# Adaptive max pooling: most loads and the large stores issued from GpSimd as one packet per DMA engine

## The chip, the core and the metric

The kernel runs on one core of a Trainium2 chip. A core has several engines with instruction streams of their own. Three matter here: VectorE (DVE in the profile) computes, SyncE (SP) only issues transfers, and GpSimd (POOL) can do both. Data moves between the device memory (HBM) and the on-chip memory (SBUF, 128 partitions) by DMA: an engine issues one instruction, and sixteen DMA engines do the copying. The profile counts what these move in packets, by queue; each issuing engine has a queue of its own (q1 is SyncE's, q10 is ScalarE's).

The metric is the device time of one execution in microseconds. The kernel before takes 335.21 us, the median of three runs (334.77 to 335.26).

## The reference

```python
x: (32, 256, 4096) float32, output_size = 256
for i in range(output_size):
    start = int(i * length / output_size)
    end = int((i + 1) * length / output_size)
    result[:, :, i] = np.max(x[:, :, start:end], axis=-1)
```

4096 / 256 is 16, so each output is the maximum of 16 neighbouring inputs. 134.2 MB are read and 8.4 MB written.

## The kernel before

All of `x` is seen as one list of 2,097,152 windows of W = 16 floats. Each of the 128 partitions handles 16,384 windows (`total`). The work is split in two groups of consecutive windows, `group_a` and `group_b`, and each group in loads. The first load is small (`FIRST`, 128 windows a partition). Then come nine loads in the first group, eight of 1024 windows a partition and one of 1020, and seven in the second, six of 1024 and one of 900. The small first load and sixteen large ones are thus seventeen loads. A load of 1024 windows is 64 KB a partition, 8 MB over all.

The loads land in one SBUF buffer, `ring`, that holds two of them and two gaps of 152 windows (`GAP`). A load's place is worked out from its number (lines 93 to 95): even loads go to the lower half, odd ones to the upper half, and every second use of a half is moved up by the gap. The maximum is taken by `pooled` (line 54), one VectorE reduce at line 56, called twice for a load: first a large part of 872 windows, then a small part of 152. The order is chosen such that the load after next, which goes to the same half but shifted, overlaps only the part that is reduced first (lines 98 to 101). It can therefore start as soon as the large part has been reduced, before the small one is.

Results are collected in the SBUF buffer `kept` until the end. They leave in three stores: one for each group from `kept`, issued by SyncE in the last lines (117), and a small one for the last load's 900 windows, whose results overwrite used places of `ring` (`last_kept`). That small one is issued by ScalarE (line 114).

The order of work on each engine is that of the source. The framework adds semaphore waits where one instruction needs another's data or place. SyncE's stream is: the small load (line 87), two large loads that wait for nothing but the start, fourteen large loads that each wait for VectorE's large reduce of the load two before (line 96), and the two stores (line 117). The first store needs nothing that is late when its turn comes; the second needs the reduces of the second group. GpSimd does four tiny memsets at the start and nothing more.

Of the kernel before, what the change touches and what calls it, by code (L numbers as in the profile page):

```python
# [1 line left out]

# [4 lines left out]


@with_exitstack
def kernel(  # L10
    ctx: ExitStack,
    tc: tile.TileContext,
    x: bass.AP,
    output_size: bass.AP,
    out: bass.AP,
):

    nc = tc.nc
    P = nc.NUM_PARTITIONS
    fp32 = mybir.dt.float32

    B, C, L = x.shape
    O = int(output_size)  # L30
    assert L % O == 0, (L, O)
    W = L // O
    total = B * C * O // P
    assert B * C * O % P == 0

    CHUNK = 1024
    GAP = 152
    FIRST = 128
    LOADS_A, LOADS_B = 9, 6

    LESS = 4
    group_a = [FIRST] + [CHUNK] * (LOADS_A - 1) + [CHUNK - LESS]
    last = total - sum(group_a) - LOADS_B * CHUNK
    group_b = [CHUNK] * LOADS_B + [last]
    assert 0 < last and last * (W + 1) <= CHUNK * W

    pool = ctx.enter_context(tc.tile_pool(name="pool", bufs=1))
    ring = pool.tile([P, 2 * (CHUNK + GAP) * W], fp32, tag="ring", name="ring")
    kept = pool.tile([P, total - last], fp32, tag="kept", name="kept")

    xw = x.flatten_outer_dims().rearrange("r (o w) -> (r o) w", w=W)
    ow = out.flatten_outer_dims().rearrange("r o -> (r o)")

    def pooled(dst, at, n):

        nc.vector.reduce_max(  # L56
            out=dst,
            in_=ring[:, at * W : (at + n) * W].rearrange("p (n w) -> p n w", w=W),
            axis=mybir.AxisListType.X,
        )  # L60

    taken = 0

    def group(n):

        nonlocal taken
        span = slice(taken * P, (taken + n) * P)
        taken += n
        return (
            xw[span].rearrange("(p n) w -> p (n w)", p=P),  # L70
            ow[span].rearrange("(p n) -> p n", p=P),
        )

    stores = []
    n_loads = 0
    base = 0
    for g, loads in enumerate((group_a, group_b)):
        xg, og = group(sum(loads))
        a = sum(loads) if g == 0 else 0
        for n in loads:  # L80
            if g == 0:
                a -= n
            xn = xg[:, a * W : (a + n) * W]
            dst = kept[:, base + a : base + a + n] if n != last else None
            if n == FIRST:

                nc.sync.dma_start(  # L87
                    out=ring[:, CHUNK * W : (CHUNK + n) * W], in_=xn
                )
                pooled(dst, CHUNK, n)  # L90
            else:

                low = n_loads % 2 * (CHUNK + GAP)
                moved = n_loads // 2 % 2
                at = low + moved * GAP
                nc.sync.dma_start(out=ring[:, at * W : (at + n) * W], in_=xn)
                if n != last:
                    cut = CHUNK - GAP if moved else GAP
                    parts = [(0, cut), (cut, n)]
                    for u, v in parts if moved else parts[::-1]:  # L100
                        pooled(dst[:, u:v], at + u, v - u)
                else:
                    end = (at + CHUNK) * W
                    last_kept = ring[:, end - n : end]
                    pooled(last_kept, at, n)
                n_loads += 1
            if g:
                a += n
        full = a - last if g else sum(loads)
        stores.append((og[:, 0:full], kept[:, base : base + full]))  # L110
        base += full
    assert taken == total

    nc.scalar.dma_start(out=og[:, full : full + last], in_=last_kept)
    tc.no_sync_barrier()
    for dst, src in stores:
        nc.sync.dma_start(out=dst, in_=src)


# [1 line left out]
_INS = ['x', 'output_size']  # L121
_OUTS = [((32, 256, 256), 'float32')]

_NUMBERS = {'output_size': 256}


# [26 lines left out]
```

## Time and profile before

| what | value |
|---|---|
| median of three runs | 335.21 us (334.77 to 335.26) |
| span of the profiled execution | 333.1 us |
| VectorE busy | 276.5 us (83%), 32 reduces |
| GpSimd busy | 0.2 us, 4 memsets |
| moved by DMA | 142.61 MB, mean 428 GB/s |
| SyncE's queue q1 | 2736 packets, 142.15 MB, 98.8% of sixteen engines' span |
| ScalarE's queue q10 | 144 packets, 0.46 MB, 0.3% |
| one large reduce, one small | 14.69 us, 2.68 us |

The profiled execution's own time is given as its span, from the first to the last thing that the profiler recorded; the runs' times also hold what lies around the span. A line of instructions names the engine, the line in the source, the operation, what is written and read, and how often. "SPq" is an issue on SyncE's queue. For a DMA issue, the time of the instruction is only that of issuing; "landing" is the time from issue until the semaphore tells that the data is there. An idle time in brackets is that of the engine just before the instruction, and behind the arrow stands what ended it.

### The profile page before, as it was taken

Reading aid. Unit: us, or ns where it says so; the run is one execution under the profiler, and the core shown is the slowest. Engines: PE = TensorE matmul, PEld = TensorE weight load, DVE = VectorE, ACT = ScalarE, POOL = GpSimd, SP = SyncE. Lnnn points to the kernel's source line nnn. Section 1 sums busy time; section 2 is a strip of 40 time slices with the busy share of each in tenths; the row PEclk is TensorE's granted clock in tenths of the full one; section 3 lists DMA queues with packets and bytes.
Section 4 is the critical chain, followed back from the end, with each engine's and each line's share of the span. In section 5 each row is a group of like instructions: output and inputs, shape, how many; then the busy total and the mean of one; then the engine's idle time right before and its main releaser. Section 6 shows DMA issues by size and latency. Waiting matters only on the chain.

```text
span 333.1 us, 113 instructions
## 1 busy us (share of the span) xinstructions
DVE 276.5 (83%) x32; POOL 0.2 (0%) x4
## 2 busy tenths in 40 slices
DVE  2009979797997979799797979979797998979993
POOL 0000000000000000000000000000000000000000
DMA  9898989899898989899898989899898989899997
GB/s 378 378 504 378 504 378 504 378 449 433 378 504 378 504 378 504 378 441 441 384 494 377 504 378 504 378 456 425 386 496 378 504 378 504 378 458 443 393 395 330
DMA packets 2880, 142.61 MB, mean 428 GB/s; under 512 B 320, under 2 KB 320, under 8 KB 448
## 3 DMA queue, kind: packets, MB, share of 16 engines
q1 hardware_dynamic: 2736, 142.15, 98.8%
q10 hardware_dynamic: 144, 0.46, 0.3%
HBM read 134.22 MB, written 8.39 MB: 428 GB/s over the span
## 4 chain that ended last, share of the span: by engine, by line
DMA 57%; DVE 36%; DVEq 5%; issue 0%; SPq 0%
DMA ring<-in_x_dram 57%; DVE kept L56 36%; DVEq L148 5%; SPq L87 0%
## 5 line engine op out<-in xcount | busy, mean ns | idle before, releaser
L56 DVE TENSOR_REDUCE kept<-ring 128x152 f32<-128x2432 f32 (+3 forms) x31 | 261.4, 8473 | 51.5 <-DMA ring<-in_x_dram 51.5
L56 DVE TENSOR_REDUCE ring<-ring 128x900 f32<-128x14400 f32 x1 | 15.1, 15143 | 0.0
L134 POOL MEMSET const-bfloat16-1.0<- 128x1 bf16 x1 | 0.1, 103 | 0.0
L134 POOL MEMSET const-uint8-127<- 128x1 uint8 x1 | 0.1, 102 | 0.0
L134 POOL MEMSET const-float32-0.0<- 128x1 f32 x1 | 0.1, 100 | 0.2 <-issue 0.2
L134 POOL MEMSET const-float32-1.0<- 128x1 f32 x1 | 0.1, 99 | 0.0
## 6 DMA issues: line engine op xcount, KB each, us to landing
ring<-in_x_dram SPq DMA_DIRECT2D x1, 8160.0 KB, 23.9
ring<-in_x_dram SPq DMA_DIRECT2D x1, 7200.0 KB, 21.7
out_dram<-kept SPq DMA_DIRECT2D x1, 4670.0 KB, 32.4
out_dram<-kept SPq DMA_DIRECT2D x1, 3072.0 KB, 18.2
ring<-in_x_dram SPq DMA_DIRECT2D x1, 1024.0 KB, 4.7
out_dram<-ring ACTq DMA_DIRECT2D x1, 450.0 KB, 4.2
ring<-in_x_dram SPq DMA_DIRECT2D x14, 24.0
```

The source lines that it names most:

```text
L56: nc.vector.reduce_max(out=dst, in_=ring[:, at * W : (at + n) * W].rearrange("p (n w) -> p n w", w=W), axis=mybir.AxisListType.X,)
L134: nc = _bacc.Bacc("TRN2", target_bir_lowering=False, num_devices=1)
L148: with _tile.TileContext(nc) as tc:
```

## The change

```diff
@@ -93,7 +93,11 @@
                 low = n_loads % 2 * (CHUNK + GAP)
                 moved = n_loads // 2 % 2
                 at = low + moved * GAP
-                nc.sync.dma_start(out=ring[:, at * W : (at + n) * W], in_=xn)
+                dst_ring = ring[:, at * W : (at + n) * W]
+                if n_loads < 2:
+                    nc.sync.dma_start(out=dst_ring, in_=xn)
+                else:
+                    nc.gpsimd.dma_start(out=dst_ring, in_=xn, single_packet=True)
                 if n != last:
                     cut = CHUNK - GAP if moved else GAP
                     parts = [(0, cut), (cut, n)]
@@ -114,7 +118,7 @@
     nc.scalar.dma_start(out=og[:, full : full + last], in_=last_kept)
     tc.no_sync_barrier()
     for dst, src in stores:
-        nc.sync.dma_start(out=dst, in_=src)
+        nc.gpsimd.dma_start(out=dst, in_=src, single_packet=True)
```

`n_loads` counts the large loads from zero. The small load and large loads 0 and 1 are still issued by SyncE. Large loads 2 to 15 and the two stores from `kept` are issued by GpSimd, with the flag that makes the share of each DMA engine one packet. Sizes, places, the reduces and the order among the moved transfers are as before; the waits of each moved instruction are the same as they were on SyncE. ScalarE's small store is unchanged.

## The prediction, made before the changed kernel was run

> **What bounds the kernel now.** I read the page first (busy shares, the slices, the queues, the chain), then the order of time on VectorE, SyncE's waits, and last the transfers stretch by stretch.
>
> From the page: its engine shares, slices, queues, chain and DMA issues.
>
> ```profile
> span 333.1 us, 113 instructions
> DVE 276.5 (83%) x32; POOL 0.2 (0%) x4
> ...
> DMA packets 2880, 142.61 MB, mean 428 GB/s; under 512 B 320, under 2 KB 320, under 8 KB 448
> ...
> q1 hardware_dynamic: 2736, 142.15, 98.8%
> q10 hardware_dynamic: 144, 0.46, 0.3%
> ...
> DMA 57%; DVE 36%; DVEq 5%; issue 0%; SPq 0%
> ...
> ring<-in_x_dram SPq DMA_DIRECT2D x14, 24.0
> ```
>
> VectorE is busy 83% of the span, so it waits; q1, SyncE's queue, is busy 98.8% of sixteen engines' time. q1 carried 19 transfers in 2736 packets, 144 each, nine per DMA engine: eight of data (the full loads' are 64 KB) and one under 512 B, which ends the transfer (320 = 20 transfers x 16 engines).
>
> The instructions in order of time (start, length, what, and in brackets the idle time before):
>
> ```profile
> 0.73 0.38 SPq L87 DMA_DIRECT2D ring<-in_x_dram  x1
> ...
> 5.44 2.29 DVE L56 TENSOR_REDUCE kept<-ring 128x128 f32<-128x2048 f32 x1 [5.44 <-DMA ring<-in_x_dram]
> 24.78 17.28 DVE L56 TENSOR_REDUCE kept<-ring 128x872 f32<-128x13952 f32 x2 [17.05 <-DMA ring<-in_x_dram]
> 44.13 17.28 DVE L56 TENSOR_REDUCE kept<-ring 128x872 f32<-128x13952 f32 x2 [2.07 <-DMA ring<-in_x_dram]
> 63.48 17.28 DVE L56 TENSOR_REDUCE kept<-ring 128x872 f32<-128x13952 f32 x2 [2.07 <-DMA ring<-in_x_dram]
> 82.83 17.28 DVE L56 TENSOR_REDUCE kept<-ring 128x872 f32<-128x13952 f32 x2 [2.08 <-DMA ring<-in_x_dram]
> ```
>
> I number the full loads 0, 1, 2 and on. They land at 24.78, 44.13, 63.48, 82.83: one each 19.35 us, with 2.07 us of VectorE idle ahead of it. A load is 8192 KB, 8.389 MB, so 433.5 GB/s. The beat is the transfer's, as long as the next load is queued before the one under way ends. Whether it is, SyncE's waits and its next issue tell:
>
> ```profile
> SPq L96 <- DVE kept L56: 205.5, 14, 14.7
> ...
> SPq L148 <- DMA out_dram<-kept: 17.8, 1, 17.8
> SPq L148 <- DMA out_dram<-ring: 1.1, 1, 1.1
> ```
>
> Fourteen loads each wait up to 14.7 us for VectorE: for the large part of the reduce of the load two before, whose place in the ring they take. Load 2 goes out at 39.49, load 1 lands at 44.13: 4.64 us of cover (the median landing of 24.0 less 19.35 says 4.65). That cover keeps the DMA engines fed:
>
> ```profile
> 63.50:295.60 232.10, 207.26 (x24) 0.00 (x0) 1.00 1.00 433
> ```
>
> This is the busy-time table by stretch; the last two columns are the DMA share and GB/s. A share of 1.00: nothing to win but what lies between packets.
>
> **The change, part by part.** The sum is made against the profiled execution: span 333.1. The runs shown are 334.77 to 335.26, median 335.21, so about 2.1 us lie outside the span.
>
> *Removed from SyncE:* fourteen load issues at 0.33 and two store issues at 0.34 and 0.43, 5.4 us in all. The chain gives SyncE's queue 0%: worth nothing.
>
> *Added to GpSimd:* the same sixteen issues with the same waits. GpSimd's queue holds four memsets done by 0.43 us, then these, so nothing else is delayed; behind each waiting load stands only the next one, which needs a later reduce. No row of this trace shows a DMA issue on GpSimd. Lower bound: SyncE's 0.33. Above: the unhidden first load took 4.71 us from issue (0.73) to reduce (5.44), of which 1.049 MB at 433 GB/s is 2.42, so 2.29 us are issue, first byte and landing together. The cover of 4.64 less 2.29 leaves 2.35: GpSimd may take about 2.3 us longer than SyncE per issue at no cost. I take SyncE's price, its row being the same instruction; beyond the cover each further microsecond is paid by fourteen loads, 14 us.
>
> *The stores:* store 0 still stands behind the last load and store 1 behind store 0. Store 1 was issued at 312.9 and began after store 0 landed (291.4 + 32.4 = 323.8): 10.9 us of cover. ScalarE's small store, 0.46 MB, lands 1.1 us after store 1 and is 1.06 us at 433 GB/s; in any order of the two the last byte comes at the same time. Zero, at most 1.1 either way.
>
> *Fewer packets:* fourteen loads and two stores go from nine packets per engine to one. A gain has little room: with the DMA share at 1.00 over 232 us, what rounding hides is half a percent, 0.005 x 288 us (125 MB moved at 433) = 1.4 us. Bounds 0 and 1.4. I take 0, because the stretch shows no gap.
>
> *The hand-over from q1 to GpSimd's queue* is the step that decides. At 39.49 load 1 has 4.64 us left on q1: about two 64 KB packets per engine (19.3/8 = 2.4 us each) and its closing packet. Until now load 2 stood behind these on the same queue. Now it comes on another, and as one packet of 8 x 64 KB, 19.3 us long. If an engine serves two queues in turn, load 2's whole packet goes ahead of load 1's rest or at least of its closing packet. Load 1 then lands with load 2, at 63.48 in place of 44.13. Its large reduce takes 14.69: load 3 can be issued at 78.2, with the engines empty since 63.4. It pays the unhidden 2.29 and 19.35 and lands at 99.8 in place of 82.83: 17.0 later. Load 2's large reduce ends at 78.18 + 2.59 + 14.69 = 95.46; load 4 is issued then, 4.4 us ahead of load 3's landing, and the old beat is back. Nothing has slack to recover the 17.0 us.
>
> The trace has one case of two queues: ScalarE's store on q10, issued at 327.99 while store 1 ran on q1. The queues' packets from 328.4 to 330.1, and from 330.6 to 332.0:
>
> ```profile
> q1 hardware_dynamic: 30, 0.74, 101.1%
> ```
> ```profile
> q10 hardware_dynamic: 113, 0.35, 63.2%
> ```
>
> q10 moved nothing until q1 was through, though from the first issue on SyncE (0.73) to the first slice with traffic takes 1.0 us, so q10 was probably ready near 329.0. So what was at most two packets and a closing packet per engine went first, which speaks for a hand-over at no cost. Yet those were 24 KB packets, 0.9 us each: the engines had taken up the rest some 1.1 to 1.6 us ahead of its end (329.0 to 330.1 and 330.6). At the hand-over load 2 is ready some 3 us ahead of load 1's closing packet, which is twice as long. Bounds: 0 and 17.0 (19.4 if the issue uses up all the cover). I take 17.0, because 3 us lies outside the lead which that row shows.
>
> The Trainium skill, "DMA: Bandwidth & Descriptors", in "Queues, rings and completion order", says that a DMA engine goes round its queues a packet at a time and finishes a whole packet first: by it the hand-over costs the 17.0 us, while the q10 row taken as plain first come, first served makes it zero. In "SBUF — State Buffer", "Who interferes with whom", it warns that VectorE's two-port modes lock out GpSimd's descriptor writing but says that a reduce never does; if it did, the small reduce right after each release would hold the issue 2.6 us, close to all the cover.
>
> **Sum:** 333.1 + 0 + 0 + 0 + 17.0 = 350.1 of span, plus 2.1 outside: 352.2.
>
> **The rivals.**
> 1. *Load 1's rest is finished first* (as the q10 row has it): the transfers follow as on one queue, all else is covered, 335.2.
> 2. *The same, and larger packets close gaps*, the other side: up to 1.4 us off the loads and stores. It decides from 0.7 us, half of the room; 333.9 to 334.5, say 334.2. For: the loads run at 433.5 and short stretches read 435. Against: the DMA share of 1.00.
> 3. *GpSimd's issue outlasts the cover*, or each transfer's end leaves a gap: from 2.3 us above SyncE's price; 1 us more is 335.2 + 14 = 349, 2 us more 363; part of the loads hit, 340. For: GpSimd never issued here. Against: half the cover spare.
> 4. *The load is cut into pieces after all* and the flag does less than it says: the two queues then alternate in 64 KB pieces, load 1's remaining 2.3 to 4.3 us double, and it lands at 46.4 to 48.4. Its large reduce ends at 61.1 to 63.1, and load 3's first byte, 2.3 later, comes at 63.4 to 65.4 against 63.5: 0 to 2 us, 336.
>
> **How the numbers follow.** Forecast 0.42 (own range 350.5 to 354.6, with the issue between SyncE's price and the whole cover), rival 1 0.14, rival 2 0.24, rival 3 0.14, rival 4 0.06. What a measurement of this kernel can tell from no change is about 0.2%, 0.67 us. Faster: rival 2, 0.24. Same: rival 1, 0.14. Slower: the rest, 0.62. The range runs from 333.9, rival 2 with nearly all of its room, to 355.0, the forecast's top; it leaves out the far part of rival 3 and the last of rival 2.
>
> **What the changed profile would show.** Right: VectorE idle once for some 17 to 20 us from about 42 us, two loads landing together near 63, a slice or so of DMA near zero from 64 to 80, then 19.35 us again; a third DMA queue with 16 transfers. Rival 1 or 2: reduces still at 44.13 and 63.48, the beat at 19.35 or up to 0.1 below. Rival 3: 2.07 of idle grown before every reduce and a DMA share below 1 in every load. Rival 4: a reduce at 46 to 48. The forecast is wrong if engines commit a queue's remaining packets well ahead of the bytes, or if GpSimd's load becomes ready only when load 1's closing packet is already under way.

## The result

The changed kernel takes 337.89 us (median of six runs, 336.73 to 338.83) against 335.09 us before: a ratio of 1.0086, 95% interval 1.0073 to 1.0098. It is slower by 2.8 us, where 17 were forecast. The profiled execution, the fastest of the six, has a span of 335.0 us against 333.1. The runs of the changed kernel also scatter over 2 us; those of the kernel before lie within 0.5.

From the page of the changed kernel: its DMA queues and GpSimd's groups of instructions.

```profile
q0 software_dynamic: 2304, 124.32, 86.1%
q1 hardware_dynamic: 432, 17.83, 12.5%
...
L100 POOL DMA_DIRECT2D ring<-in_x_dram x14 | 7.5, 538 | 285.6 <-DVE kept L56 285.6
L121 POOL DMA_DIRECT2D out_dram<-kept x2 | 1.1, 536 | 21.0 <-DVE kept L56 21.0
```

GpSimd's queue q0 moved its sixteen transfers in 2304 packets, 144 each: nine per DMA engine, as on SyncE's queue, with the flag set. So the flag did not make one packet of an engine's share.

The changed kernel's instructions in order of time around the hand-over (start, length, what, idle time before):

```profile
24.73 17.28 DVE L56 TENSOR_REDUCE kept<-ring 128x872 f32<-128x13952 f32 x2 [17.14 <-DMA ring<-in_x_dram]
39.72 0.67 POOL L100 DMA_DIRECT2D ring<-in_x_dram  x1 [39.28 <-DVE kept L56]
46.60 34.47 DVE L56 TENSOR_REDUCE kept<-ring 128x872 f32<-128x13952 f32 x4 [4.59 <-DMA ring<-in_x_dram]
61.60 0.53 POOL L100 DMA_DIRECT2D ring<-in_x_dram  x1 [21.21 <-DVE kept L56]
78.77 0.53 POOL L100 DMA_DIRECT2D ring<-in_x_dram  x1 [16.64 <-DVE kept L56]
84.20 17.28 DVE L56 TENSOR_REDUCE kept<-ring 128x872 f32<-128x13952 f32 x2 [3.14 <-DMA ring<-in_x_dram]
```

Load 1 lands at 46.60 in place of 44.13, 2.5 us late. Load 2 has landed by the time VectorE is done with load 1. Load 3 lands at 84.20 in place of 82.83, 1.4 us late. The sixteen DMA engines had to wait for it. Their busy shares from 62 to 64 us, in slices of 0.05 us, and the queue's packets, in the kernel before:

```profile
DMA  0000000000009099999909000000000000000000
...
q1 hardware_dynamic: 32, 1.05, 121.3%
```

and in the changed kernel:

```profile
DMA  0000000000000000009090999090009000999900
...
q0 software_dynamic: 32, 1.05, 151.2%
```

The view books a whole packet in the slice where it starts. Both stretches hold the sixteen closing packets of load 2 and the sixteen first pieces of load 3, 64 KB each. Before, they start together from 62.6 to 63.1. In the changed kernel load 2's last pieces had started nearly as early (from 60.2 us on in both), but load 3's first pieces start only from 62.9 to 63.9, some 1.6 to 2.6 us after its place was released at 46.60 + 14.69 = 61.29. They are slower too: by the share in the last column a piece takes 3.0 us (2 us x 1.512) in place of 2.4.

Of the 1.9 us of span, 1.4 are there by load 3. Another 0.5 comes later, in steps of 0.25 us and less: the last full load lands at 297.51 against 295.62. From there to the end it is 37.5 us in both kernels (333.1 - 295.62 and 335.0 - 297.51), so the tail with the two moved stores costs nothing.

GpSimd issues later and longer than SyncE. Load 3's place is released at 61.29; the issue starts at 61.60 and takes 0.53. On SyncE it started 0.02 after the release and took 0.33. GpSimd is done with issuing 0.5 us later.

Two numbers serve below. The **cover** of a load is the time from the release of its place to the landing of the load before it. The **need** is the time from release to its own landing, less the time the transfer takes at full rate (19.35 us). A load is late when its need exceeds its cover. In the kernel before the cover is 44.13 - (24.78 + 14.69) = 4.66.

### The profile page after: what moved, and what is told of

Same layout as the page of the kernel before. It is cut to its first block, busy times and chain, and to the rows that moved or that the text cites. A ratio compares the mean times of both kernels' runs of the same rounds, so it can differ in the third digit from the quotient of the medians.

```text
span 335.0 us, 115 instructions
## 1 busy us (share of the span) xinstructions
DVE 276.4 (83%) x32; POOL 8.8 (3%) x20
## 3 DMA queue, kind: packets, MB, share of 16 engines
q0 software_dynamic: 2304, 124.32, 86.1%
## 4 chain that ended last, share of the span: by engine, by line
DMA 56%; DVE 37%; DVEq 5%; issue 1%; SPq 0%
DMA ring<-in_x_dram 56%; DVE kept L56 37%; DVEq L152 5%; SPq L98 0%; SPq L87 0%
## 5 line engine op out<-in xcount | busy, mean ns | idle before, releaser
L100 POOL DMA_DIRECT2D ring<-in_x_dram x14 | 7.5, 538 | 285.6 <-DVE kept L56 285.6
L121 POOL DMA_DIRECT2D out_dram<-kept x2 | 1.1, 536 | 21.0 <-DVE kept L56 21.0
```

The costliest lines, as they stand in the source:

```text
L100: nc.gpsimd.dma_start(out=dst_ring, in_=xn, single_packet=True)
L121: nc.gpsimd.dma_start(out=dst, in_=src, single_packet=True)
```

## The experiments

Loads are numbered as in the prediction. Ratios are of mean times, to the kernel before, run on the same chip.

**How a DMA engine shares its time between queues, and what the flag does.** Load 1 alone is moved to GpSimd, so that two full loads start side by side:

```diff
-                nc.sync.dma_start(out=ring[:, at * W : (at + n) * W], in_=xn)
+                if n_loads != 1:
+                    nc.sync.dma_start(out=ring[:, at * W : (at + n) * W], in_=xn)
+                else:
+                    nc.gpsimd.dma_start(out=ring[:, at * W : (at + n) * W], in_=xn, single_packet=True)
```

> The kernel before, but load 1 alone is issued from GpSimd, with the flag, at the start, beside the small load and load 0 on SyncE. Both queues then have work from about 2.7 us on. Theory A (turns at every 64 KB piece): the small load's last 8 KB pieces alternate with pieces of load 1 and it is reduced at 10 to 15 us; load 1 lands at 30 to 35, load 0 near 44. Theory B (one packet is not interrupted): load 1's 19.3 us run through, it lands at 22 to 24, and the small load only about then. If a queue's earlier transfers simply go first: small load at 5.4, load 0 at 24.8, load 1 at 44.

> As the run with load 1 alone from GpSimd, without the flag. Theory A: the same landings as with the flag, within 1 us. Theory B: the landings differ by many us, load 1 later than with the flag.

The queues' packets from 12 to 24 us, with the flag:

```profile
q0 software_dynamic: 44, 2.88, 55.8%
q1 hardware_dynamic: 32, 2.10, 40.7%
```

and without:

```profile
q0 software_dynamic: 39, 2.56, 49.2%
q1 hardware_dynamic: 36, 2.36, 45.4%
```

Each is 64 KB a packet. From 12 to 36 us the two queues move about the same: 76 packets on q0 and 80 on q1 with the flag, 72 and 80 without. VectorE's first large reduce starts at 44.65 with the flag and at 44.24 without: two loads that share the engines from 5.4 us on land together after 2 x 19.35 us, at 44.1. So the engines take turns at every 64 KB piece, and the flag does not hold the eight pieces together. (The small load was not caught in this, since load 1's first piece came too late: it was reduced at 5.4.) That is theory A for the two full loads; the landing that I gave load 1, 30 to 35, was too early, as it rested on an earlier start. Theory B, on which the forecast of 17 us rested, is out. The order of work changed with it (at the end a full load is reduced at 333.74, behind the small last one at 311.71), so the whole time (362.6 and 362.3 us) says nothing on the case.

The flag taken off the changed kernel alone:

```diff
-                    nc.gpsimd.dma_start(out=dst_ring, in_=xn, single_packet=True)
+                    nc.gpsimd.dma_start(out=dst_ring, in_=xn)
...
-        nc.gpsimd.dma_start(out=dst, in_=src, single_packet=True)
+        nc.gpsimd.dma_start(out=dst, in_=src)
```

> The changed kernel without the one-packet flag; all else as changed. Theory A (a DMA engine takes turns between queues at every 64 KB piece, flag or not, so the flag does nothing here): load 1 lands 2 to 3 us late (46.6 to 47 in place of 44.1), the beat afterwards is 19.35 to 19.6, and the time is that of the changed kernel, 336.7 to 338.8. Theory B (the flag does bind the pieces together and costs or saves something): the median differs from 337.9 by more than 1 us, or load 1 lands elsewhere than 46 to 47.

338.11 us (336.98 to 339.73), ratio 1.0098, interval 1.0066 to 1.0129: the changed kernel's time and spread. Load 1 lands at 46.64, and the packets are 144 a transfer here too.

With turns of one piece, the hand-over reads as follows. q0's and q1's packets in the changed kernel from 44 to 47 us:

```profile
q0 software_dynamic: 16, 1.05, 80.7%
q1 hardware_dynamic: 5, 0.00, 0.1%
```

The five packets without bytes on q1 are closing packets of load 1: eleven of its sixteen had gone before, five waited while their engine moved one piece of load 2, some 2.4 us. Load 1's data was not held up: its last pieces had started by 41.4, and load 2's first ones start from 43.3 on. Load 1 has landed only when the last of the sixteen is through.

**Is it the hand-over or GpSimd?** The same hand-over to ScalarE in place of GpSimd; the last small store changes to SyncE so that it does not block the large ones:

```diff
-                    nc.gpsimd.dma_start(out=dst_ring, in_=xn, single_packet=True)
+                    nc.scalar.dma_start(out=dst_ring, in_=xn)
...
-    nc.scalar.dma_start(out=og[:, full : full + last], in_=last_kept)
+    nc.sync.dma_start(out=og[:, full : full + last], in_=last_kept)
...
-        nc.gpsimd.dma_start(out=dst, in_=src, single_packet=True)
+        nc.scalar.dma_start(out=dst, in_=src)
```

> The changed kernel with loads 2 to 15 and the two large stores issued from ScalarE in place of GpSimd (no flag), and the small last store from SyncE in place of ScalarE. The same hand-over between two queues at load 2, but issued as SyncE issues. Theory A (hand-over costs a turn, GpSimd's late readiness costs the rest and makes the spread): load 1 lands 2 to 5 us late, load 3 1 to 2.5 us late, afterwards every load 19.35 us as before; 336.2 to 337.6 with runs within 0.5 us. Rival (the hand-over costs nothing by itself and everything lost comes from GpSimd): 335.1, load 1 at 44.1.

337.33 us (337.18 to 337.98), ratio 1.0075, interval 1.0058 to 1.0092. Its instructions in order of time:

```profile
46.55 34.46 DVE L56 TENSOR_REDUCE kept<-ring 128x872 f32<-128x13952 f32 x4 [4.58 <-DMA ring<-in_x_dram]
85.01 17.28 DVE L56 TENSOR_REDUCE kept<-ring 128x872 f32<-128x13952 f32 x2 [3.99 <-DMA ring<-in_x_dram]
```

Load 1 is as late as with GpSimd, load 3 even later (2.2 us). Most of the loss is had without GpSimd. Load 3's need here is 85.01 - (46.55 + 14.69) - 19.35 = 4.4 us; in the changed kernel 84.20 - 61.29 - 19.35 = 3.6. The prediction had taken 2.3 from the very first load.

The other way round, GpSimd without a costly hand-over: only the small load on SyncE, or nothing.

```diff
-                if n_loads < 2:
+                if n_loads < 0:
```

> The changed kernel with the hand-over moved to the front: only the small load stays on SyncE, all sixteen large loads and both large stores come from GpSimd with the flag. There the small load's last pieces are 8 KB and VectorE has nothing else to do. Theory (only the hand-over between two queues with 64 KB pieces costs; GpSimd as issuer costs nothing): load 1 at 44 to 45, load 3 19.35 after load 2, 335.0 to 335.8, and runs within 0.5 us. Rival (part of the loss, and the spread of 2 us over the runs, are GpSimd's): 335.8 to 337.5 with single loads 0.2 to 0.6 us late.

335.29 us (334.94 to 337.92), ratio 1.0025, interval 1.0010 to 1.0040; seven of twelve runs lie below 335.4, five at 336.2 to 337.9. In the profiled one (337.92) loads are late by 0.1 to 0.7 here and there. So the hand-over at load 2 makes up most of the changed kernel's loss, but the scatter does not go with it: the rival was right in that.

For the next one, line 87 is changed to GpSimd as well, with the flag.

> All seventeen loads and both large stores from GpSimd with the flag; no hand-over among loads at all. Theory: the beat as in the kernel before, the start later by what GpSimd needs more for its first transfer, 0.3 to 1.0 us: 335.3 to 336.3. Rival (GpSimd's issue is late for some loads): 336 to 338.

336.31 us (336.02 to 336.92), ratio 1.0044, interval 1.0032 to 1.0056. The small load lands at 6.14 in place of 5.44, so 0.7 us of the 1.4 is the later start; in the profile three of the first eight loads come 0.2 late, later ones hardly.

**How much cover is needed.** GAP 100 in place of 152 makes the large reduce, and with it the release, 0.86 us later (15.55 us in place of 14.69). In the changed kernel and in the kernel before:

```diff
-    GAP = 152
+    GAP = 100
```

> The changed kernel with GAP 100 in place of 152: the large reduce grows by 52 windows, 0.88 us by 14.69 us for 872, and every load is issued 0.88 us later in the transfer before it; the hand-over stays. Theory (GpSimd's load is ready 1.6 to 2.6 us after its place is released, as load 3 showed): the cover is still 3 us or more, so 0 to 2 us more than the changed kernel, 337.9 to 340. Rival (GpSimd's readiness uses up the whole cover already, so the spread comes from there): 0.3 to 0.9 us more on most of thirteen loads, 342 to 349.

> The kernel before with GAP 100, all loads from SyncE: the same 0.88 us less cover without GpSimd and without a hand-over. Theory: the cover of 4.6 us goes to 3.8 us and stays enough, 335.0 to 335.5. If SyncE's load needs more than about 3 us from issue to its first piece while the engines are busy, each load is late by 0.1 to 0.4 us: 336 to 340.

Both became slower, and both theories failed: 345.11 us (343.62 to 346.34), ratio 1.0303, interval 1.0277 to 1.0329, and 339.47 us (336.53 to 339.88), ratio 1.0116, interval 1.0085 to 1.0146. VectorE in the kernel before with GAP 100, all on SyncE, one queue:

```profile
63.69 17.28 DVE L56 TENSOR_REDUCE kept<-ring 128x924 f32<-128x14784 f32 x2 [2.28 <-DMA ring<-in_x_dram]
83.03 17.28 DVE L56 TENSOR_REDUCE kept<-ring 128x924 f32<-128x14784 f32 x2 [2.06 <-DMA ring<-in_x_dram]
102.78 17.28 DVE L56 TENSOR_REDUCE kept<-ring 128x924 f32<-128x14784 f32 x2 [2.47 <-DMA ring<-in_x_dram]
122.14 17.28 DVE L56 TENSOR_REDUCE kept<-ring 128x924 f32<-128x14784 f32 x2 [2.08 <-DMA ring<-in_x_dram]
142.34 17.28 DVE L56 TENSOR_REDUCE kept<-ring 128x924 f32<-128x14784 f32 x2 [2.92 <-DMA ring<-in_x_dram]
```

Every second load or so is late, by 0.2 to 1.0 (2.07 of idle is the even beat), with a cover of 44.13 - (24.78 + 15.55) = 3.8. A late load adds its lateness to the cover of the next one, which is then on time. So SyncE's need while the engines are busy is often above 3.8: 4.0 to 4.8 for the late loads. Of the 4.66 us of cover in the kernel before, less than 0.86 is spare. GpSimd takes 0.5 us of it by issuing later: 0.86 us less cover costs SyncE 4.5 us and the changed kernel 7.2.

**Later is not worse.** The two reduces of load 0 are exchanged, so that load 2 is released 2.6 us later and misses load 1's closing packets:

```diff
-                    for u, v in parts if moved else parts[::-1]:
+                    for u, v in parts if moved or n_loads == 0 else parts[::-1]:
```

> The changed kernel with the two reduces of load 0 in the other order, the small one first, so that load 2's place comes free at 42.0 in place of 39.4, 2.6 us later; nothing else moves. Theory (the hand-over costs because load 2's first piece takes an engine's turn ahead of load 1's closing packet): load 2 is now ready only at about 44, load 1 lands at 44.1 to 44.4 on time, load 2 starts 0.3 to 1.5 us late, load 3 is at most 1.5 us behind the kernel before; 335.8 to 337.2, faster than the changed kernel although a load is issued later. Rival (late issue is what costs): 2 us or more slower than the changed kernel, 339 to 341.

The changed kernel was run again beside it:

> The changed kernel once more, on the same chip as the three beside it: 336.7 to 338.9, load 1 at 46 to 47.

336.77 us (336.61 to 337.22), ratio 1.0056, interval 1.0043 to 1.0069, against 337.77 us (337.11 to 340.63), ratio 1.0112, interval 1.0081 to 1.0143, for the changed kernel (load 1 at 46.49). With the late issue:

```profile
42.27 0.67 POOL L100 DMA_DIRECT2D ring<-in_x_dram  x1 [41.83 <-DVE kept L56]
44.10 17.28 DVE L56 TENSOR_REDUCE kept<-ring 128x872 f32<-128x13952 f32 x2 [2.14 <-DMA ring<-in_x_dram]
59.09 0.53 POOL L100 DMA_DIRECT2D ring<-in_x_dram  x1 [16.16 <-DVE kept L56]
65.53 17.28 DVE L56 TENSOR_REDUCE kept<-ring 128x872 f32<-128x13952 f32 x2 [4.16 <-DMA ring<-in_x_dram]
```

Load 1 is on time at 44.10, so the turn was what held it up. Load 2 is then 2.05 us late, more than the 1.5 I allowed, with a need of 65.53 - 41.96 - 19.35 = 4.2. The medians favour the late issue by 1 us; the two profiled executions are alike (spans 335.4 and 335.3), so I take it as no worse, not as a gain.

**Twice.** A second hand-over, back to SyncE from load 8 on, the stores too:

```diff
-                if n_loads < 2:
+                if n_loads < 2 or n_loads >= 8:
...
-        nc.gpsimd.dma_start(out=dst, in_=src, single_packet=True)
+        nc.sync.dma_start(out=dst, in_=src)
```

> The changed kernel with a second hand-over: large loads 2 to 7 from GpSimd, 8 to 15 and the two large stores from SyncE again. Theory (each hand-over costs a turn, 1.4 to 2.5 us): load 7 lands 2 to 3 us late as load 1 does, 339 to 341 in all. Rival (the loss is spread over GpSimd's fourteen loads): fewer of them, so 336.5 to 337.5, less than the changed kernel.

338.24 us (338.03 to 338.58), ratio 1.0099, interval 1.0085 to 1.0112: 0.5 us above the changed kernel beside it, which is not clear of that kernel's scatter. The time lies between the two expectations.

```profile
142.67 17.28 DVE L56 TENSOR_REDUCE kept<-ring 128x872 f32<-128x13952 f32 x2 [2.28 <-DMA ring<-in_x_dram]
...
164.53 34.40 DVE L56 TENSOR_REDUCE kept<-ring 128x872 f32<-128x13952 f32 x4 [4.58 <-DMA ring<-in_x_dram]
201.25 17.28 DVE L56 TENSOR_REDUCE kept<-ring 128x872 f32<-128x13952 f32 x2 [2.32 <-DMA ring<-in_x_dram]
```

Load 7 is 2.5 us late, as at the first hand-over, but load 9 comes 201.25 - 142.67 - 3 x 19.35 = 0.5 us late only: SyncE's need was 2.7 this once. The turn was the same at both hand-overs; what it cost differed with the need of the load after.

**ScalarE at the front.** The hand-over behind the small load, with ScalarE in place of GpSimd (the edits of the ScalarE run and `n_loads < 0`):

> The hand-over at the front as before (only the small load on SyncE), but all large loads and large stores come from ScalarE in place of GpSimd, and the small last store from SyncE. Theory (a hand-over behind 8 KB pieces is free, and ScalarE issues at SyncE's price): 334.8 to 335.3, every run within 0.5 us, load 1 at 44.1. If it shows runs up to 338 as the same kernel from GpSimd did, that spread is not GpSimd's.

This expectation failed: 337.32 us (335.39 to 338.82), ratio 1.0067, interval 1.0045 to 1.0090. In the profiled run, the fastest, the small load lands only at 22.93, its 8 KB pieces taking turns with 64 KB ones of load 0 (from 12 to 18 us, 32 packets of each queue); VectorE has nothing else to do then, and the loads follow at 19.35 us from 44.69 on. Of the slower runs there is no trace. What it shows is that the scatter is not GpSimd's alone, and that ScalarE's loads can lose as much without the hand-over at load 2 (337.32) as with it (337.33). Where the slower runs lose it is not known.

**More cover.** Loads of 970 windows and a gap of 203, one load more in the second group. The transfer takes 18.33 us and the large reduce 12.92, so the cover in the even beat grows from 4.65 to 5.4:

```diff
-    CHUNK = 1024
-    GAP = 152
+    CHUNK = 970
+    GAP = 203
...
-    LOADS_A, LOADS_B = 9, 6
+    LOADS_A, LOADS_B = 9, 7
```

> The kernel before with smaller loads and a larger gap (CHUNK 970, GAP 203, one load more in the second group): a load takes 18.33 us and the large reduce before its release 12.92, so the cover grows from 4.65 to 5.4 us. The kernel before lost nothing to late loads, so nothing is won: 334.8 to 335.6.

> The same sizes with all large loads and large stores from GpSimd and only the small load on SyncE (no costly hand-over). Theory (what is left of the loss without the hand-over, and its spread, is cover that GpSimd's later and longer issue takes away, 0.4 us of it): with 0.76 us more cover no load is late; 334.9 to 335.7 and every run within 0.5 us, where the same kernel with the old sizes spread from 334.9 to 337.9. Rival (GpSimd's transfers are slower by themselves): the spread stays.

> The same sizes with the changed kernel's hand-over at load 2. Theory: load 1 still lands 2.3 us late by one piece of load 2, 0.76 us of it absorbed by the larger cover, no other load late: 335.8 to 336.8, runs within 0.6 us. Rival (the hand-over is not what costs): 335.0 as without it.

| with the larger cover | median, runs | ratio, interval |
|---|---|---|
| all on SyncE | 335.03 us, 334.92 to 335.14 | 1.0002, 0.9992 to 1.0011 |
| small load on SyncE, the rest on GpSimd | 335.02 us, 334.88 to 336.29 | 1.0004, 0.9996 to 1.0013 |
| the change, hand-over at load 2 | 335.01 us, 334.82 to 335.40 | 1.0001, 0.9992 to 1.0010 |

GpSimd's loss is gone, and so is its scatter but for one run of eleven. The hand-over's loss is gone too, where I had expected 0.8 to 1.8 us of it to stay. In the last of these kernels:

```profile
44.32 32.66 DVE L56 TENSOR_REDUCE kept<-ring 128x767 f32<-128x12272 f32 x4 [4.29 <-DMA ring<-in_x_dram]
57.57 0.53 POOL L100 DMA_DIRECT2D ring<-in_x_dram  x1 [20.00 <-DVE kept L56]
73.84 0.53 POOL L100 DMA_DIRECT2D ring<-in_x_dram  x1 [15.74 <-DVE kept L56]
78.86 16.38 DVE L56 TENSOR_REDUCE kept<-ring 128x767 f32<-128x12272 f32 x2 [1.87 <-DMA ring<-in_x_dram]
```

and, for load 3, in the one with all on SyncE:

```profile
78.79 16.38 DVE L56 TENSOR_REDUCE kept<-ring 128x767 f32<-128x12272 f32 x2 [1.93 <-DMA ring<-in_x_dram]
```

Load 1 is late as before (44.32; with all on SyncE it lands at 42.06), so the turn is still taken. But load 3 lands at 78.86 against 78.79 on SyncE: its release at 57.24 leaves it enough. That is 78.86 - 57.24 - 18.33 = 3.3 us beside the transfer, less than the 3.8 that were too little in the GAP 100 run, so the need is no single number. The turn moves bytes of load 2 ahead and wastes nothing by itself; it costs only what load 3 lacks in cover. These sizes change the loads and their pieces (60.6 KB in place of 64) along with the cover; GAP 100 left the loads as they were. None of these kernels beats the one before, which leaves the DMA engines no gap to fill.

## Why the prediction was wrong

**What bounds the kernel** was read rightly: the transfers' beat, kept up by issuing each load ahead of the end of the last. Direction and place were right too: load 1 late, then load 3.

**The step that failed is the hand-over**, taken at 17.0 us because the flag was taken to make one packet of 19.3 us. That load 1's closing packet may wait behind load 2 was right; the length of the turn was not. The packet count per transfer stayed 144, and the engines changed queues after one 64 KB piece, some 2.4 us. Load 1 was 2.5 us late and not 19.3, load 3 1.4 and not 17.0. Load 2 was also not ready some 3 us ahead of load 1's closing packets: eleven of these sixteen still went first.

**Rival 4**, to which I gave 0.06, has the turn right, and its numbers come near: load 1 at 46.4 to 48.4 (measured 46.60), a cost of 0 to 2 us, the time 336 (measured 337.89). In part that is luck. Load 1's data did not alternate with load 2's; only closing packets waited. And by rival 4's own working, with 2.3 us from release to first byte, load 1 at 46.60 would make load 3's first byte come at 61.29 + 2.29 = 63.58 against 63.5, about 0.1 us late. It was 1.4 late, because load 3's need was 3.6.

**The q10 row** was read with a wrong readiness. I took ScalarE's store to be ready at 329.0 by the 1.0 us that the first issue took on idle engines. In the run with ScalarE at the front, load 0 was issued at 0.73 beside SyncE's small load, and fifteen of its sixteen first pieces started at 3.0 us or later, 2.3 us and more after the issue. For the store, issued at 327.99, that would be 330.3; q10's first packets came from 330.2 on, when the last pieces on q1 were through. So that row showed no queue going first and no lead.

**The cover** was called half spare, since the first load's issue, first byte and landing took 2.29 us together. On busy engines the need is 2.7 to 4.4 us after a hand-over, and 4.0 to 4.8 for the late loads of the GAP 100 run. The term "GpSimd may take about 2.3 us longer than SyncE per issue at no cost" should have been less than 0.86, and rival 3 belonged into the sum at small size: GpSimd without the hand-over at load 2 still lost 0.25% (interval 0.10 to 0.40). That this accounts for all the rest of the loss is not shown. That it is cover which GpSimd takes, and not slower transfers, is what the runs with more cover speak for: there GpSimd's loads took SyncE's time.

**GpSimd's issue**, costed at SyncE's 0.33, is 0.53 and starts 0.3 us later. **The stores** cost nothing, as predicted. **Fewer packets** won nothing, as taken, but because there were no fewer packets.

**The Trainium skill's rule** in "DMA: Bandwidth & Descriptors", "Queues, rings and completion order", that a DMA engine goes round its queues a packet at a time, agrees with the turns seen here. The 9 to 17 descriptors that the page calls typical for a packet do not: a turn was one 64 KB piece, one of the nine packets that the profile counts per engine, and the flag left it so. The page's "Specifications" name about 0.6 us to the first byte for SyncE and ScalarE and about 1 us for GpSimd. On idle engines the first traffic came 1.0 us after SyncE's issue began (0.73 to 1.7, kernel before) and 1.4 us after GpSimd's (1.26 to 2.7, all loads from GpSimd): both longer, and as far apart. The needs measured here are longer still; they hold busy engines and the landing as well. In "SBUF — State Buffer", "Who interferes with whom", the page says that a reduce does not block GpSimd's descriptor writing; with cover enough GpSimd's loads ran beside the reduces at SyncE's time (335.02 against 335.03 us), which agrees.

**What stays open:** why the need varies from one load to the next, and why load 3's first pieces took 3.0 us. Also where the changed kernel's slower runs lose, since its profiles are of its fastest executions: of the median's 2.8 us, 1.9 are seen in the trace. The run without the flag has a trace of a slower execution (338.3 us): load 3 is 2.1 us late there, and four later loads 0.1 to 0.7 each.

## What to carry to other kernels

Before moving part of a stream of transfers to another queue, look at what is still under way on the old one: here an engine changed queues at each 64 KB piece, and the last, smallest packet of the older transfer, which everything waited for, stood behind a piece of the newer. Measure the time from release to landing in the running loop, by a run with slightly less lead, and not on the first transfer, when the engines are idle. Where lead is short, a loop sized for more of it made both the queue and the issuing engine indifferent.

## What the runs showed that I had not expected

- The one-packet flag changed neither the number of packets in the records (144 a transfer) nor the turns between queues.
- 0.86 us less lead cost 4.5 us over fourteen loads in a kernel that, by its first load, seemed to have 2.3 us to spare.
- A load issued 2.6 us later did not make the kernel slower (336.77 against 337.77 us).
- On ScalarE and SyncE side by side, a 1 MB load in 8 KB pieces landed at 22.9 us in place of 5.4, because each of its pieces took turns with a 64 KB one.
